# Gated DeltaNet recurrence by two groups of four heads, its beta item fifth, and the planner's clock without the residual's affine

## The chip, the cores and the metric

The kernel runs on one core of a Trainium2 chip. The metric is the device time of one execution in microseconds; three runs of the kernel before gave 1348.18, 1348.34 and 1351.75, median 1348.34. The engines are TensorE (PE, with its weight loads PEld), VectorE (DVE), ScalarE (ACT), GpSimd (POOL) and SyncE (SP). Each runs its own instructions in order and waits on semaphores for the others.

## The reference

A trunk of two layers over 512 tokens of width 1024. Layer 0 has a gated linear attention mixer, layer 1 a gated DeltaNet mixer (the one that the change touches); each is followed by a ConvFFN, and every sublayer by a LayerNorm of `ALPHA * h + f(h)`.

```python
def gdn_mixer(x, w_in, conv_w, a_log, dt_bias, norm_w, w_out):
    proj = x @ w_in
    qkv, gate, beta_lin, a_lin = jnp.split(...)
    qkv = silu(causal_dwconv(qkv, conv_w))            # 4 taps
    q, k, v = ...                                     # 8 heads of 128; q, k l2-normalized
    beta = sigmoid(beta_lin)
    g = -exp(a_log) * softplus(a_lin + dt_bias)       # per head and token
    o = rms_norm(gdn_chunked(q, k, v, beta, g), norm_w)
    return (o * silu(gate)) @ w_out

# gdn_chunked, chunk by chunk:
#   S_t = exp(g_t) (I - beta_t k_t k_t^T) S_{t-1} + beta_t k_t v_t^T ;  o_t = S_t^T q_t
```

The kernel uses chunks of 128 tokens, so the recurrence has four steps (`ck`) for each of eight heads (`hd`).

## The kernel before, in words

All activations of 512 tokens stay on the chip; weights stream in from DRAM as pieces of 128x1024, in the order of a list (`plan`), through the SP queue. ACT casts each to `wh` (L231), DVE subtracts to get the rest `wl` (L232), and each product of two fp32 matrices is three matmuls (wh with xh and xl, wl with xh).

The mixer's input projection comes first, as *items*: one item is 128 output channels by 512 tokens, 24 matmuls into one bank (`fm`). The first `HEADSTART` = 4 items are done in two halves of 256 tokens, while the LayerNorm of the last tokens is not ready; the rest is done whole. Items of the second mixer before: the beta/a item (`ba`), then q and k of head 0, 1, ... 7, then v of heads 0 to 7. Behind them come the *gates* (`tm`: tokens on the partitions, two halves `hf` of four heads, 96 matmuls each) and the output projection.

What follows an item:
- q, k, v: `gdn_conv`, one tap on ACT (L889), three on DVE (L891), Silu on ACT (L892). Then a transpose on PE (tile `qkT` or `vT`, L161), and for q and k the sums of squares on ACT (L970, into `gd_ssq`).
- beta/a (`ba_done`): Exp, softplus and a running sum (L915 to L925, ACT and DVE in turns), a store of the sums to DRAM (`drow`, L927), and eight broadcast loads from it, one per head (`dt`, L930), both on POOL's queue. `decays` then transposes beta (`bat`), subtracts on DVE (L948, four per head) and exponentiates on ACT (L953).
- `qk_task` goes on with k^T k, k^T q and the matrix `am`; `base` (two groups of four heads) inverts the triangular matrices on DVE (L1017, L1019) and PE, into `rm`.

`chain` is the recurrence. Before, one task per head, each step with 128-column operations in two shared banks, `ca` and `cb`, and a slot `cc`: transpose of k, k times state, `yy` (L1144, DVE), times `rm`, scaling (L1148, ACT), q times state, state update (L1161, DVE), output (L1163, L1164, DVE), sum of squares (L1165, ACT). Head h waits for head h - 2 at the same step, so heads run in pairs. At the last head of each step `r2` (an inverse root, L387 to L393) is made for all heads. The chains were spawned behind all items, so they ran in the gates and after them. `finish` multiplies the gated output (`sg`, L1187), and `split_y` transposes it (`yT`) for the output projection. `unspill` loads the residual `h` back and applies the last LayerNorm's affine to it on DVE (L572, L573).

The order is not written out: the parts are Python generators that are resumed by `pump` between matmuls, when a planner's clock (`clk`, advanced by each matmul's assumed cost) has passed their due time; `vec(cost)` books DVE time in that clock, and `yield t` asks to be resumed t later. `until` waits for a flag. LayerNorm's transposes (`xT`) are due when the booked DVE time is over. PE's order is fixed to the program's; a scheduler places the rows of the other engines.

Of the kernel before, what the change touches and what calls it, by code (L numbers as in the profile page):

```python
# [15 lines left out]
P = 128  # L16
# [33 lines left out]
class Trunk:  # L50
# [504 lines left out]
    def unspill(self, gb_rows):  # L555
# [339 lines left out]
    def gdn(self, li, g, b):  # L895
# [70 lines left out]
        def qk_task(t, hd, which):  # L966
            pt = self.psum("qkT")
            self.tr4(pt, t)
            for ck in range(4):
                nc.scalar.activation(pt[:, blk(ck)], pt[:, blk(ck)], AF.Square,  # L970
                                     accum_out=ssq[:, which, hd, ck:ck + 1])
            if which == 0:
                return
# [115 lines left out]
        def v_done(ps, hd):  # L1089
            if hd == 0:  # L1090
                x = self.small([P, 64], "gd_x")
                rs = self.small([P, 64], "gd_rs")
                nc.vector.tensor_scalar_add(x, ssq.rearrange("p a h c -> p (a h c)"), RMS_EPS)
                nc.vector.tensor_copy(rk, x[:, 32:].rearrange("p (h c) -> p h c", h=DH))
                self.rsqrt(rs, x, 64)
                nc.vector.tensor_copy(rr, rs[:, :32].rearrange("p (h c) -> p h c", h=DH))
                nc.vector.tensor_mul(rk, rk, rs[:, 32:].rearrange("p (h c) -> p h c", h=DH))
# [3 lines left out]
        def v_task(t, hd):  # L1101
            pt = self.psum("vT")
            self.tr4(pt, t)
            v[hd] = vt = self.slot("v")
            for ck in range(4):
                nc.scalar.mul(vt[:, blk(ck)], pt[:, blk(ck)], rk[:, hd, ck:ck + 1])
# [3 lines left out]
        items = [ba_done]  # L1110
        for hd in range(DH):
            for which in range(2):
# [3 lines left out]
        for hg in range(2):  # L1116
            self.spawn(base(hg))
        self.fm_items(items)


        ss, r2 = keep("gd_ss"), keep("gd_r2")
        sg = [[None, None] for _ in range(NTB)]
        y = [[None, None] for _ in range(NTB)]
        st = [self.slot("state"), self.slot("state")]

        def chain(hd):
            yield from self.until(("v", hd))
            yield from self.until(("rm", hd))
            yield from self.until("decays")
            s = st[hd // 4][:, blk(hd % 4)]  # L1130
            for ck in range(4):
                if ck and hd == 0:
                    yield from self.until(("chain", DH - 1, ck - 1))
                elif hd > 1:
                    yield from self.until(("chain", hd - 2, ck))
                sl = blk(ck)
                vv = v[hd][:, sl]
                pa = self.psum("ca")
                cc = self.slot("cc")
                yy, vn, kd = cc[:, blk(0)], cc[:, blk(1)], cc[:, blk(2)]  # L1140
                self.tr(pa[:, blk(0)], k[hd][:, sl])
                if ck > 0:
                    self.mm(pa[:, blk(1)], k[hd][:, sl], s)
                    nc.vector.scalar_tensor_tensor(yy, pa[:, blk(1)], neb[:, hd, ck:ck + 1], vv, ALU.mult, ALU.add)  # L1144
                nc.scalar.mul(kd, pa[:, blk(0)], ebl[:, hd, ck:ck + 1])
                yield 1.0
                self.mm(pa[:, blk(2)], rm[hd][:, sl], yy if ck else vv)
                nc.scalar.mul(vn, pa[:, blk(2)], bp[:, hd, ck:ck + 1])  # L1148
                pb = self.psum("cb")
# [127 lines left out]
```

## Time and profile before

| what | us |
|---|---|
| three runs | 1348.18, 1348.34, 1351.75 |
| profiled execution, its own time | 1347.16 |
| its span on the core | 1345.4 |
| mean granted TensorE clock | 0.988 of full speed |
| PE busy | 1302.7 |
| DVE busy | 826.6 |
| ACT busy | 551.9 |

Times below are those of the profiled execution, counted from the start of its span. The second mixer begins at about 609 us (first `fm` matmul of its head start) and ends at about 966, where the second ConvFFN's first matmul runs. A timeline row has start, duration, engine, line, operation, output<-inputs, shapes, count, and in brackets how long the engine stood idle before it and on what. Rows of the same kind in a row are joined, with their count.

### The profile page before, as it was taken

To read this page: it belongs to the slowest core of one execution; us is meant where nothing else is said; L and a number is where in the kernel's file an instruction comes from. 1 tells how busy PE (TensorE), PEld (TensorE's weight loads), DVE (VectorE), ACT (ScalarE), POOL (GpSimd) and SP (SyncE) were. 2 spreads that over 40 slices of the span, in tenths; PEclk is the share of its full clock that TensorE was granted. 3 is DMA by queue.
4 is the path that set the end of the run, shared out by engine and by line. 5 is a ranking of instruction groups with operands and counts; after the bars stand their busy time and mean duration, and the time that the engine had idled before them with its cause. 6 is when DMAs were issued, how large, how long until landed. Compare 5 with 4: busy or idle time off the path is not lost. (4 is left out here: it accounts for less than half of the span.)

```text
span 1345.4 us, 17426 instructions
## 1 busy us (share of the span) xinstructions
PE 1302.7 (97%) x6686; PEld 1078.5 (80%) x6686; DVE 826.6 (61%) x1570; ACT 551.9 (41%) x1036; POOL 118.6 (9%) x162
## 2 busy tenths in 40 slices
PE   9999999999999999998999989988899999999996
PEld 8688888988888888887787768877788888888885
DVE  3853466676533555566779894679667553355546
ACT  4644443634421344426565344553444431244420
POOL 3000000070000000001032301010025000000000
PEclk9999999999999999999999999998999999999998
DMA  6321223143223333432432322143143323333331
GB/s 188 95 78 54 72 93 111 53 131 99 94 94 95 94 94 94 122 115 87 121 93 68 87 79 77 49 141 93 34 125 94 95 94 94 96 94 94 94 109 63
DMA packets 165172, 126.38 MB, mean 94 GB/s; under 512 B 13992, under 2 KB 137706, under 8 KB 165088
## 3 DMA queue, kind: packets, MB, share of 16 engines
q1 hardware_dynamic: 159984, 115.10, 28.9%
q0 software_dynamic: 4240, 8.60, 2.1%
q10 hardware_dynamic: 864, 1.57, 0.3%
q8 instruction: 52, 0.85, 0.2%
q14 instruction: 32, 0.26, 0.1%
HBM read 119.46 MB, written 5.78 MB: 93 GB/s over the span
## 5 line engine op out<-in xcount | busy, mean ns | idle before, releaser
L232 DVE TENSOR_TENSOR wl<-raw,wh 128x1024 fp32r<-128x1024 f32 (+1 forms) x191 | 239.2, 1254 | 338.7 <-ACT wh L231 337.8
L150 PE MATMUL fm<-xh,wh 128*128 128x512 f32 (+1 forms) x1104 | 412.2, 374 | 0.3 <-ACT wh L231 0.3
L150 PE MATMUL fm<-xl,wh 128*128 128x512 f32 (+1 forms) x1104 | 408.5, 370 | 0.2 <-DVE xl L526 0.2
L150 PE MATMUL fm<-xh,wl 128*128 128x512 f32 (+1 forms) x1104 | 407.5, 370 | 0.0
L231 ACT CAST wh<-raw 128x1024 fp32r<-128x1024 f32 (+1 forms) x191 | 199.3, 1044 | 296.7 <-PE tm L150 161.2
L150 PEld LDWEIGHTS fm<-xh,wh 128*128 128x128 f32 x1104 | 208.8, 189 | 40.9 <-issue 2.3
L150 PEld LDWEIGHTS fm<-xh,wl 128*128 128x128 f32 x1104 | 208.3, 189 | 38.3 <-DVE wl L232 0.2
L150 PEld LDWEIGHTS fm<-xl,wh 128*128 128x128 f32 x1104 | 208.9, 189 | 36.9 <-DVE xl L526 0.4
L601 DVE SCALAR_TENSOR_TENSOR conv<-fm,ffn_cw,conv 128x511 f32<-128x511 f32 (+1 forms) x176 | 130.7, 746 | 3.0
L150 PE MATMUL tm<-wh,gh 128*128 128x512 f32 x288 | 112.1, 389 | 0.0
L150 PE MATMUL tm<-wl,gh 128*128 128x512 f32 x288 | 112.1, 389 | 0.0
L150 PE MATMUL tm<-wh,gl 128*128 128x512 f32 x288 | 112.1, 389 | 0.0
L150 PE MATMUL tm<-wh,xh 128*128 128x512 f32 x192 | 81.0, 422 | 0.0
L378 ACT CAST gh<-conv 128x512 fp32r<-128x512 f32 x44 | 27.3, 621 | 123.9 <-DVE conv L616 123.7
L150 PE MATMUL tm<-wh,xl 128*128 128x512 f32 x192 | 76.3, 397 | 0.0
L150 PE MATMUL tm<-wl,xh 128*128 128x512 f32 x192 | 75.7, 394 | 0.0
L611 ACT ACTIVATE conv<-conv 128x512 f32<-128x512 f32 x44 | 27.8, 632 | 92.5 <-DVE conv L601 92.5
L150 PEld LDWEIGHTS tm<-wh,gl 128*128 128x128 f32 x288 | 54.1, 188 | 11.3
L150 PEld LDWEIGHTS tm<-wh,gh 128*128 128x128 f32 x288 | 54.1, 188 | 11.3
L150 PEld LDWEIGHTS tm<-wl,gh 128*128 128x128 f32 x288 | 54.1, 188 | 11.2
L599 ACT ACTIVATE conv<-fm,ffn_cw 128x512 f32<-128x512 f32 x88 | 59.9, 681 | 0.1
L540 POOL TENSOR_TENSOR h<-h,gb 128x512 f32<-128x512 f32 x16 | 27.1, 1718 | 359.4 <-DMA gb<-in_ln_g_dram 359.4
(262 smaller groups left out, 1659.0 us busy)
## 6 DMA issues: line engine op xcount, KB each, us to landing
raw<-in_ffn_w_in_dram SPq DMA_DIRECT2D x88, 512.0 KB, 3.7
raw<-in_ffn_w_out_dram SPq DMA_DIRECT2D x44, 512.0 KB, 3.6
raw<-in_gdn_w_in_dram SPq DMA_DIRECT2D x32, 512.0 KB, 4.1
raw<-in_gla_w_in_dram SPq DMA_DIRECT2D x24, 512.0 KB, 3.6
raw<-in_gla_w_out_dram SPq DMA_DIRECT2D x8, 512.0 KB, 3.5
raw<-in_gdn_w_out_dram SPq DMA_DIRECT2D x8, 512.0 KB, 3.8
hd<-h POOLq DMA_DIRECT2D x8, 256.0 KB, 2.5
dt<-drow POOLq DMA_DIRECT2D x8, 256.0 KB, 7.0
```

The costliest lines, as they stand in the source:

```text
L150: t = self.nc.tensor.matmul(out, a, b, start=start, stop=stop)
L231: nc.scalar.copy(wh[:, cols], raw[:, cols])
L232: nc.vector.tensor_sub(wl[:, cols], raw[:, cols], wh[:, cols])
L378: cast = self.nc.scalar.copy(dst_h, src)
L540: nc.gpsimd.tensor_mul(h[hf], h[hf], gb[hf])
L599: nc.scalar.activation(a, ps, AF.Identity, scale=tap(2))
L601: nc.vector.scalar_tensor_tensor(a[:, d:], ps[:, :S - d], tap(2 - d), a[:, d:], ALU.mult, ALU.add)
L611: nc.scalar.activation(a, a, AF.Gelu)
```

## The change

Four edits:
1. The beta/a item is the fifth: the head start holds q and k of heads 0 and 1, and beta is done whole behind them.
2. `chain` is one task for a group of four heads. Each operation of a step is done for the four heads in a whole bank of its own (`ks`, `vn`, `kT`, `qs`, `s`, `o`), so the copies and additions are 512 columns wide, and k's transposes are left out in the last step. A group's task waits for its own heads alone; it is spawned ahead of the items, so that group 0 can start when v of heads 0 to 3 and their `rm` are there.
3. `r2` and the normalizers `rk`, `rr` are made per group (new flags `ssq`, `rk`, `r2`), and `finish` for half hf needs `r2` of group hf only.
4. `unspill`'s affine books no DVE time in the planner (`self.vec(1.4)` is gone).

```diff
-                    self.vec(1.4)
                     self.set(("h", tb, hf))
...
     def gdn_plan(self, w_in, w_out):
-        self.plan_pad([(w_in, 4096, 8, 0), (w_in, 4104, 8, H0)])
         for hd in range(DH):
+            if hd == HEADSTART // 2:
+                self.plan_pad([(w_in, 4096, 8, 0), (w_in, 4104, 8, H0)])
...
+            self.set(("ssq", which, hd))
...
         def v_done(ps, hd):
-            if hd == 0:
...
             t = self.gdn_conv(ps, 16 + hd)
             self.spawn(v_task(t, hd), 4.5)
         def v_task(t, hd):
+            g, h = divmod(hd, 4)
+            hs4 = slice(4 * g, 4 * g + 4)
+            if h == 0:
+                for i in range(4 * g, 4 * g + 4):
+                    yield from self.until(("ssq", 0, i))
+                    yield from self.until(("ssq", 1, i))
...
+                v[g] = [self.slot("v") for _ in range(4)]
+                self.set(("rk", g))
+            else:
+                yield from self.until(("rk", g))
...
+        def chain(g):
+            heads = [(blk(h), 4 * g + h) for h in range(4)]
+            for _, hd in heads:
+                yield from self.until(("v", hd))
+                yield from self.until(("rm", hd))
+            yield from self.until("decays")
+            s = self.slot("state")
+            for ck in range(4):
+                sl, one = blk(ck), slice(ck, ck + 1)
+                vv = yy = v[g][ck]
+                if ck > 0:
+                    ps = self.psum("ks")
+                    for w, hd in heads:
+                        self.mm(ps[:, w], k[hd][:, sl], s[:, w])
+                    yy = self.slot("yy")
+                    for w, hd in heads:
+                        nc.vector.scalar_tensor_tensor(yy[:, w], ps[:, w], neb[:, hd, one], vv[:, w],
+                                                       ALU.mult, ALU.add)
+                    yield 1.2
+                ps = self.psum("vn")
+                for w, hd in heads:
+                    self.mm(ps[:, w], rm[hd][:, sl], yy[:, w])
+                vn = self.slot("vn")
+                for w, hd in heads:
+                    nc.scalar.mul(vn[:, w], ps[:, w], bp[:, hd, one])
+                if ck < 3:
+                    ps = self.psum("kT")
+                    kd = self.slot("kd")
+                    for w, hd in heads:
+                        self.tr(ps[:, w], k[hd][:, sl])
+                    for w, hd in heads:
+                        nc.scalar.mul(kd[:, w], ps[:, w], ebl[:, hd, one])
+                if ck > 0:
+                    ps = self.psum("qs")
+                    for w, hd in heads:
+                        self.mm(ps[:, w], q[hd][:, sl], s[:, w])
+                    for w, hd in heads:
+                        nc.vector.tensor_scalar_mul(vv[:, w], ps[:, w], eb[:, hd, one])
+                yield 1.4
+                if ck < 3:
+                    ps = self.psum("s")
+                    for w, hd in heads:
+                        self.mm(ps[:, w], kd[:, w], vn[:, w])
+                    if ck == 0:
+                        nc.vector.tensor_copy(s, ps)
+                    else:
+                        for w, hd in heads:
+                            nc.vector.scalar_tensor_tensor(s[:, w], s[:, w], cd[:, hd, one], ps[:, w],
+                                                           ALU.mult, ALU.add)
+                ps = self.psum("o")
+                for w, hd in heads:
+                    self.mm(ps[:, w], pj[hd][:, sl], vn[:, w])
+                if ck == 0:
+                    nc.vector.tensor_copy(vv, ps)
+                else:
+                    nc.vector.tensor_add(vv, vv, ps)
+                for w, hd in heads:
+                    nc.scalar.activation(vn[:, w], vv[:, w], AF.Square, accum_out=ss[:, hd, one])
+                yield 1.2
...
+        def finish(tb, hf):
+            yield from self.until(("sg", tb, hf))
+            yield from self.until(("r2", hf))
...
-        items = [ba_done]
+        items = []
         for hd in range(DH):
+            if hd == HEADSTART // 2:
+                items.append(ba_done)
...
         for hg in range(2):
             self.spawn(base(hg))
+            self.spawn(chain(hg))
         self.fm_items(items)
...
-        for hd in range(DH):
-            self.spawn(chain(hd))
```

What this does to the order, at three places. The first is DVE's queue around the `dt` rows. Before, where the transposed beta (`gd_bt`) has been read and `dt_4970` (head 0) comes up; the `conv` there is k of head 1, and the convolutions of q0, k0 and q1 stand earlier:

```order
L976 RECIPROCAL gd_bp_4775<-gd_bp_4775 128x4
L977 TENSOR_TENSOR gd_bp_4775<-gd_bp_4775,gd_bt_4779 128x4
L978 TENSOR_SCALAR gd_bn_4774<-gd_bp_4775 128x4
L232 TENSOR_TENSOR wl_5203<-raw_5200,wh_5202 128x1024
L891 SCALAR_TENSOR_TENSOR conv_5148<-fm_5097,gdn_cw_177,conv_5148 128x511
L948 TENSOR_SCALAR dt_4970<-dt_4970,gd_bt_4779 128x128
L891 SCALAR_TENSOR_TENSOR conv_5148<-fm_5097,gdn_cw_177,conv_5148 128x510
```

And now (`dt_5141` and `dt_5143` are heads 0 and 1, `conv_5188` is q of head 2, `conv_5242` k of head 2):

```order
L925 SCALAR_TENSOR_TENSOR ba_4778<-reset_79,z_5129 8x512
L937 COPY gd_bt_4777<-bat_5219 128x256
L939 TENSOR_SCALAR gd_bt_4777<-gd_bt_4777 128x4x8
L940 RECIPROCAL gd_bt_4777<-gd_bt_4777 128x4x8
L978 TENSOR_TENSOR gd_bp_4773<-gd_bp_4773,gd_bt_4777 128x4 x2
L979 TENSOR_SCALAR gd_bn_4772<-gd_bp_4773 128x4 x2
L232 TENSOR_TENSOR wl_5297<-raw_5294,wh_5296 128x1024
L948 TENSOR_SCALAR dt_5141<-dt_5141,gd_bt_4777 128x128 x4
L948 TENSOR_SCALAR dt_5143<-dt_5143,gd_bt_4777 128x128 x4
L891 SCALAR_TENSOR_TENSOR conv_5188<-fm_5163,gdn_cw_177,conv_5188 128x511
L891 SCALAR_TENSOR_TENSOR conv_5242<-fm_5200,gdn_cw_177,conv_5242 128x511
L891 SCALAR_TENSOR_TENSOR conv_5188<-fm_5163,gdn_cw_177,conv_5188 128x510
```

The scan that feeds `drow`, and so the copies into `dt`, stands only a few rows ahead of the first row that reads `dt`, and two convolutions stand behind it. On PE the transpose of `conv_5188` (q2) follows the item of k2.

The second place is the end of the recurrence on DVE. Before, the roots of the last two steps (`gd_rs`, `rs_t`) for all heads, interleaved, and the products into `sg` of one token block (`sg_7118`) behind it:

```order
L392 TENSOR_TENSOR rs_t_1166_7533<-rs_t_1166_7533,gd_rs_1165_7529 128x8
L387 TENSOR_SCALAR gd_rs_1178_7596<-gd_x_1177_7595 128x8
L393 SCALAR_TENSOR_TENSOR gd_rs_1165_7529<-rs_t_1166_7533,gd_rs_1165_7529 128x8
L388 TENSOR_SCALAR gd_rs_1178_7596<-gd_rs_1178_7596 128x8
L389 TENSOR_SCALAR gd_x_1177_7595<-gd_x_1177_7595 128x8
L1177 SCALAR_TENSOR_TENSOR gd_r_1017_6653<-gd_rs_1165_7529,gd_rr_4778 128x8
L391 TENSOR_TENSOR rs_t_1179_7600<-gd_rs_1178_7596,gd_x_1177_7595 128x8
L1187 SCALAR_TENSOR_TENSOR sg_7118<-v_6147,gd_r_1017_6653,sg_7118 128x128
L1187 SCALAR_TENSOR_TENSOR sg_7118<-v_6335,gd_r_1017_6653,sg_7118 128x128
```

And now, the second half's gates (`sg_7594` to `sg_7616`), where no step and no root is left between the gate and its products:

```order
L232 TENSOR_TENSOR wl_7663<-raw_7660,wh_7662 128x1024
L647 TENSOR_TENSOR sg_7594<-sg_7594,gdn_nw_180 128x512
L1206 SCALAR_TENSOR_TENSOR sg_7594<-v_6578,gd_r_802_4785,sg_7594 128x128 x2
L647 TENSOR_TENSOR sg_7603<-sg_7603,gdn_nw_180 128x512
L1206 SCALAR_TENSOR_TENSOR sg_7594<-v_6578,gd_r_802_4785,sg_7594 128x128 x2
L1206 SCALAR_TENSOR_TENSOR sg_7603<-v_6579,gd_r_802_4785,sg_7603 128x128
L647 TENSOR_TENSOR sg_7616<-sg_7616,gdn_nw_180 128x512
```

The root of group 1 (L1196) stands seven rows ahead of `sg_7594`'s first, with four of the second half's weight casts between; the last product of group 1 stands on PE in the gates' first half.

The third place is PE at the end of the mixer. Before, the LayerNorm's transposes stand together ahead of the ConvFFN's first item (`fm_8279`):

```order
L161 MATMUL xT_8175<-ident_72,h_7735 128x128 x4
L161 MATMUL xT_8207<-ident_72,h_7727 128x128 x4
L161 MATMUL xT_8219<-ident_72,h_7737 128x128 x4
L161 MATMUL xT_8231<-ident_72,h_7729 128x128 x4
L161 MATMUL xT_8243<-ident_72,h_7739 128x128 x4
L161 MATMUL xT_8255<-ident_72,h_7731 128x128 x4
L161 MATMUL xT_8267<-ident_72,h_7741 128x128 x4
L150 MATMUL fm_8279<-xh_82,wh_7981 128x256
```

And now, where the transposes of the last token block (`xT_8194`, `xT_8212`) stand inside the second item:

```order
L150 MATMUL fm_8181<-xl_83,wh_7888 128x256
L161 MATMUL xT_8194<-ident_72,h_7642 128x128 x4
L150 MATMUL fm_8181<-xh_82,wl_7889 128x256
L161 MATMUL xT_8212<-ident_72,h_7652 128x128 x4
L150 MATMUL fm_8181<-xh_82,wh_7888 128x256
```

The other six stand still earlier, between the output projection's last tiles; all of the ConvFFN behind is in the same order as before.

More of the change, by code (lines that the diff above doesn't have):

```diff
@@ L1089, in v_done @@
         def v_done(ps, hd):
-            if hd == 0:
[L1091 to L1097, printed above, removed]
             t = self.gdn_conv(ps, 16 + hd)
@@ L1181, in finish @@
-        def finish(tb, hf):
-            yield from self.until(("sg", tb, hf))
-            yield from self.until(("r2", 3 if (hf or tb > 1) else tb))
-            t = sg[tb][hf]
-            for hd in range(4 * hf, 4 * hf + 4):
-                w = blk(hd % 4)
-                nc.vector.scalar_tensor_tensor(t[:, w], v[hd][:, blk(tb)], r2[:, hd, tb:tb + 1], t[:, w],
-                                               ALU.mult, ALU.mult)
-            yield 1.2
-            self.split_y(y, tb, hf, t)
-            self.set(("y", tb, hf), 1.5)
@@ L1198, in gdn @@
         self.gates(self.gdn_nw, P, sg)
-        self.wait(("r2", 3))
+        self.wait(("r2", 1))
         self.unspill(spilled)
```

95 lines of the change are left out of this document (36 added, 59 removed).

## The prediction

> **What bounds the kernel now.** I read the page's busy shares first, then the waits of the TensorE queue (PE) by releaser, then windows over the stretch from 600 to 1000 us, where the second mixer lies, and last the timelines of single rows there.
>
> ```profile
> PE 1302.7 (97%) x6686; PEld 1078.5 (80%) x6686; DVE 826.6 (61%) x1570; ACT 551.9 (41%) x1036; POOL 118.6 (9%) x162
> ```
>
> PE is busy 97% of the span. A change that leaves its matmuls alone can only win back idle or slow PE time, or lose more. From 590 to 1000 us PE waited for these (waiter, releaser, us in total, times, longest):
>
> ```profile
> PE qkT L161 <- ACT conv L892: 9.8, 3, 7.8
> PE yT L161 <- DVE sg L1187: 7.2, 2, 3.8
> PE vT L161 <- ACT conv L892: 4.3, 6, 1.0
> PE xT L161 <- DVE h L509: 4.0, 1, 4.0
> ```
>
> Four places: the first q and k transposes wait for their convolutions, the v transposes for theirs, the output's transposes (yT) for the recurrence, and the next feed-forward block (xT) for LayerNorm. The same by windows (us; busy time of PE, PEld, DVE, ACT, POOL; granted clock; DMA share; GB/s):
>
> ```profile
> 666.00:750.00 84.00, 81.97 (x440) 68.41 (x438) 75.50 (x195) 46.82 (x133) 22.46 (x42) 1.00 0.34 89
> 750.00:814.00 64.00, 58.37 (x445) 46.29 (x445) 55.02 (x125) 27.11 (x62) 9.27 (x17) 0.97 0.29 81
> 814.00:889.00 75.00, 75.00 (x622) 65.32 (x621) 42.45 (x131) 37.48 (x117) 6.87 (x14) 1.00 0.23 67
> 889.00:922.00 33.00, 24.91 (x130) 21.05 (x129) 30.50 (x114) 16.28 (x47) 4.81 (x9) 0.84 0.29 89
> ...
> 960.00:970.00 10.00, 5.93 (x37) 5.46 (x36) 7.44 (x22) 10.00 (x28) 0.00 (x0) 0.83 0.00 0
> ```
>
> VectorE (DVE) is busy 86 to 90% up to 814 us and only 57% in the gates (814 to 889), where PE never pauses. After the last gate matmul the recurrence is left over: PE idles 8.1 of 33 us and runs the rest at a clock of 0.84.
>
> **Durations used.** Starts that follow each other give the price of a row:
>
> ```profile
> 889.03 0.39 PE L150 MATMUL tm<-wl,xh 128*128 128x512 f32 x1
> 889.26 0.39 PE L150 MATMUL tm<-wh,xl 128*128 128x512 f32 x1
> 889.49 0.27 PE L161 MATMUL ca<-ident,conv 128*128 128x128 f32 x1
> 889.60 0.39 PE L150 MATMUL ca<-state,conv 128*128 128x128 f32 x2
> 889.82 0.27 PE L161 MATMUL ca<-ident,conv 128*128 128x128 f32 x1
> ```
>
> A 512-column matmul costs 0.23 us, a transpose 0.11, a plain fp32 128-column product 0.22 (it shows as two records). The new recurrence has the same 136 products and 24 transposes for 32: **0.9 us** of PE work less. Everything else is about waits.
>
> **Part 1, the beta item fifth.** Before, PE stood still until the first convolution's Silu, because beta's work came first on ACT and DVE:
>
> ```profile
> 633.50 1.04 ACT L231 CAST wh<-raw 128x1024 fp32r<-128x1024 f32 x1 [1.25 <-PE fm L150]
> 641.42 1.12 PE L161 MATMUL qkT<-ident,conv 128*128 128x128 f32 x4 [7.84 <-ACT conv L892]
> 642.76 0.63 PE L150 MATMUL fm<-xl,wh 128*128 128x512 f32 x1
> 643.19 0.63 PE L150 MATMUL fm<-xh,wl 128*128 128x512 f32 x1
> 662.44 0.60 PE L161 MATMUL qkT<-ident,conv 128*128 128x128 f32 x4
> ```
>
> The four head-start items end at 633.5; then 7.8 us idle, and six matmuls at 0.43 for 0.23, another 1.2. The row at 662.44 is q2's transpose, behind the items beta, q0, k0, q1, k1, q2, k2. In the changed order the same seven items lie ahead of q2's transpose, so that row is the place to compare.
>
> After, the head start (q0, k0, q1, k1) ends at 633.5 as well; q0's convolution has nothing ahead of it, and PE goes on with the transposes (4 groups of 0.45) and the beta item (24 x 0.23 = 5.6), with some 0.6 of short stalls: beta is done at about 641.4, where PE was just waking before. So far 8 to 9 us are gained. Then beta's chain runs. Its prices:
>
> ```profile
> 639.44 1.28 ACT L892 ACT_TABLE_LOAD   x1 [3.04 <-DVE conv L891]
> 627.31 0.59 ACT L915 ACTIVATE ba<-fm 8x512 f32<-8x512 f32 x1
> 627.91 0.68 ACT L917 ACTIVATE z<-fm,gdn_al 8x512 f32<-8x512 f32 x1
> 629.69 0.63 ACT L919 ACTIVATE na<-na 8x512 f32<-8x512 f32 x1
> 630.35 0.72 ACT L920 ACTIVATE na<-na,one 8x512 f32<-8x512 f32 x1
> 643.15 0.26 ACT L970 ACTIVATE qkT<-qkT 128x128 f32<-128x128 f32 x1
> 643.56 0.26 ACT L970 ACTIVATE qkT<-qkT 128x128 f32<-128x128 f32 x1
> 661.66 0.63 ACT L892 ACTIVATE conv<-conv 128x512 f32<-128x512 f32 x1 [2.48 <-DVE conv L891]
> ...
> 631.11 0.68 DVE L921 SCALAR_TENSOR_TENSOR z<-z,na 8x512 f32<-8x512 f32 x1 [0.19 <-ACT na L920]
> 631.90 0.47 DVE L924 TENSOR_SCALAR z<-z,gd_ea 8x512 f32<-8x512 f32 x1
> 632.48 1.21 DVE L925 TENSOR_TENSOR_SCAN ba<-reset,z 8x512 f32<-8x512 f32 x1
> 636.00 6.25 DVE L891 SCALAR_TENSOR_TENSOR conv<-fm,gdn_cw,conv 128x511 f32<-128x511 f32 x9
> 655.49 2.83 DVE L948 TENSOR_SCALAR dt<-dt,gd_bt 128x128 f32<-128x128 f32 x14
> ...
> 633.98 0.52 POOL L927 DMA_DIRECT2D drow<-ba  x1 [17.57 <-DVE ba L925]
> 636.32 4.25 POOL L930 DMA_DIRECT2D dt<-drow  x8 [1.82 <-issue]
> ...
> dt<-drow POOLq DMA_DIRECT2D x8, 256.0 KB, 7.0
> ```
>
> On ACT between 641.4 and the Ln: two table loads (2.6), L915, L917, L919, L920 (2.6), four L970 squares (0.41 apart, 1.6) and one weight cast (1.04), about 8 us with the hand-overs: 649.4. DVE adds L921, L924 and the scan, 2.5: **652**. Before, the scan ended at 633.69 and the second dt copy was issued at 636.32 + 0.53; with the median 7.0 to landing that is 643.9, 10.2 after the scan. After: 662.2.
>
> That wait was free before: the first L948 ran at 653.8, ten microseconds after the landing. After, the built order puts the eight L948 of the first two heads **ahead** of q2's and k2's convolutions on DVE. So: 662.2, four L948 (0.2 each, 0.8), five of six interleaved convolution rows (6.25/9 = 0.69 each, 3.5), Silu's table load 1.28 and Silu 0.63: q2 is ready at **668.4**. PE has only two items (11.2) and beta's transposes (which wait a little for the scan) to fill: it is through at about 653.5, and idles 15 us. Against 662.44 the change is 6.0 late there, plus again 1.2 at the low clock: **+7**. Behind the stall on DVE stand everything for k2 and q3; ACT's wait for q2 also holds the casts of the next weights, but those two are in hand.
>
> The Trainium skill, "DMA: Bandwidth & Descriptors", section "Latency and other measured facts", puts the fixed cost of a DMA at about 2 us. Two in a row would by that be near 4 us plus transfer, and q2 some 4 to 6 us sooner, +2 instead of +7. The trace has 7.0 for the second alone, eight being in flight at once, and the sum goes by the trace. The page "ScalarE: Activation LUTs", section "What ACT_TABLE_LOAD costs", gives 2.66 us for a table switch, load and drain; the three on this path would add 4 us. Here the Silu starts at 640.74, 1.30 after the load's start, so I count 1.3 each.
>
> Bounds for this part: -9 if q2 is not late at all; if only ACT's queue holds it (copies landed in time), the stall is about 7 and -2 is left; if the two copies land as late as the eighth (issued 3.7 later), +11. I take the walk's +7.
>
> **Part 2, the recurrence in two groups.** Group 0 now runs among the v items, group 1 in the first half of the gates. The prices of its DVE rows, 128 wide:
>
> ```profile
> L1163 DVE TENSOR_SCALAR v<-cb,gd_eb 128x128 f32<-128x128 f32 x8 | 2.8, 346 | 0.5 <-PE cb L150 0.4
> L1144 DVE SCALAR_TENSOR_TENSOR cc<-ca,gd_neb,v 128x128 f32<-128x128 f32 x7 | 2.4, 347 | 0.7 <-PE ca L150 0.6
> ```
>
> A group has 32 such rows (12 yy, 12 scalings, 8 state updates) at about 0.3 between starts, and 5 of 512 columns at 0.6: 13 us of DVE. It goes into the v items, which were already the tight stretch (750 to 814 above: DVE 55 and PE 58 busy of 64, PE idle 5.6). Summed row by row in the built order, from v0's convolution to v6's: DVE 65.8, PE 62.2; before, over v0 to v7, they were even (54 and 55). So DVE bounds there by 3.6, and each step's yy stands behind convolutions and weight casts in DVE's queue, some 2 more: **+5.5**. Ends: 0 (PE's matmuls of the group, 15.5 us, fill the idle) and +13 (the group's whole DVE time). I take the value nearer to the sums.
>
> In the gates each wide step has six 512-column matmuls (1.4) between its parts: four yy on DVE take 1.2 plus a hand-over, eight ACT scalings 2.1 against 2.7 of PE work. Nearly covered: **+1** over some 12 hand-overs.
>
> What it buys is the tail. The recurrence ends in the gates' first half, and yT of the second half needs only its own gate: 5.5 us of matmuls lie between that gate's last product and its transpose, against ACT 0.7, one 512-wide and four 128-wide DVE rows, 3.3. The 8.1 idle us of 889 to 922 go, and the low clock with them (0.16 of the 24.9 busy, 4.0), and about 1.5 of transposes that ran at half pace: **-13.5**; next late there is the output's weights, with DMA at 0.29.
>
> **Part 3, the residual's booked time.** The planner now starts LayerNorms earlier, so the xT transposes stand between the last output tiles and the head start. Of the 4.05 idle and the 0.83 clock behind it (10 us x 0.17 x 0.6 busy, 1.0) I count **-4.5**, at worst 0.
>
> **Sum:** -0.9 + 7 + 5.5 + 1 - 13.5 - 4.5 = **-5.4** against the profiled run's 1347.16 (its span 1345.4 and 1.8 around it); that run lies 1.2 under the median 1348.34. Predicted median: 1348.3 - 5.4 = 1342.9, call it **1342.5**. What a measurement here can tell from no change is 0.3%, 4.0 us.
>
> **Rivals.** (a) The dt copies do not hold q2: they land early, or the low end of part 1 holds. Speaks for it: 2.5 us of the 10.2 are issue. Then part 1 gives -9 to +2 and the sum is 1327 to 1338, with -2 likeliest: 1334. (b) Slower: the v items become bound by DVE's queue. PE, in order, waits at each of 12 hand-overs of group 0 for a row that stands behind a 2.1 us convolution and a 1.2 us cast. At 1.5 us each 18 in place of 6.5, so 1354; it decides from the point where DVE's sum passes PE's by 10 us, and the sums say 3.6. (c) No change: the tail keeps half of its wait, because the output's weights or the second gate half come late: -7 for -13.5, 1349. (d) The wide group is not through by the second gate half, since its base (the triangular inverses) ends later than before and its blocks come by DMA; then the tail merely moves, 1356.
>
> **How the numbers follow.** Forecast 0.45 (1338 to 1348), (a) 0.22, (b) 0.13, (c) 0.14, (d) 0.06. Faster by over 0.3% (under 1344.3): (a) and two thirds of the forecast, 0.53; within: a third of the forecast and most of (c), 0.28; slower (over 1352.4): 0.19. The range reaches from within (a) to just past (b): 1329 to 1355; outside stay the far ends of (a) and (d).
>
> **What would show it.** In the changed trace: PE idle before q2's transpose of 12 to 17 us with the convolutions of q2 behind L948 on DVE (right), or under 7 (wrong: part 1). DVE over 95% busy and PE idle 10 to 14 us between v0 and v7. No wait of yT over 1 us and a clock near 1.0 after the gates. xT waiting under 1.5 us. The forecast fails if beta's chain on ACT is much shorter than 11 us or dt lands within 6 us of the scan.

## The result and the profile after

| | before | after |
|---|---|---|
| median of the compared runs, us | 1348.59 | 1338.36 |
| lowest and highest, us | 1348.18, 1351.75 | 1334.57, 1338.54 |
| profiled execution, us | 1347.16 | 1338.32 |

The ratio is 0.9921, 95% interval 0.9898 to 0.9944: the changed kernel is faster, by 10.2 us between the medians. The sign was forecast and the time lies in the range, but the gain is nearly twice the forecast (10.2 for 5.4).

The changed kernel's page begins so (span; then busy time, share of the span and instructions of each engine):

```profile
span 1336.6 us, 17354 instructions
PE 1297.8 (97%) x6678; PEld 1074.2 (80%) x6678; DVE 818.2 (61%) x1526; ACT 548.3 (41%) x1030; POOL 118.5 (9%) x162
```

PE has eight instructions fewer and is still busy for 97%; its busy time fell by 4.9, more than the eight transposes (0.9) cost; the windows below show one place where the rest went, matmuls that now run at the full clock. The waits of PE from 590 to 1000 us (waiter, releaser, us in total, times, longest):

```profile
PE qkT L161 <- ACT conv L892: 17.1, 6, 11.5
PE R L150 <- DVE V L1060: 1.6, 1, 1.6
PE bat L161 <- DVE ba L925: 1.3, 1, 1.3
PE V L150 <- DMA T<-dinvt: 1.2, 2, 0.9
PE vT L161 <- ACT conv L892: 0.9, 2, 0.7
PE xT L161 <- DVE ln_t L494: 0.5, 1, 0.5
PE xT L161 <- DVE h L509: 0.5, 2, 0.3
```

The waits of yT (7.2 before) are gone, those of xT fell from 4.0 to 1.0 and those of vT from 4.3 to 0.9. The wait of the q and k transposes *grew*, from 9.8 to 17.1, and bat, R and V (beta's transpose and the inversions) wait for 4.1 where before only R did, for 1.3. The windows of the mixer (columns as in the prediction):

```profile
672.00:753.00 81.00, 76.81 (x405) 63.91 (x405) 67.59 (x187) 42.10 (x120) 20.16 (x35) 0.99 0.27 69
753.00:817.00 64.00, 58.69 (x478) 48.72 (x476) 59.46 (x153) 28.64 (x76) 12.25 (x25) 0.95 0.30 79
817.00:892.00 75.00, 74.59 (x632) 65.67 (x633) 50.45 (x153) 39.17 (x134) 10.80 (x20) 1.00 0.31 91
892.00:925.00 33.00, 33.00 (x153) 27.17 (x152) 24.33 (x46) 11.73 (x19) 0.00 (x0) 1.00 0.31 99
```

The gates reach 908.1 now, so 892 to 925 is their end and the start of the output projection with the yT transposes: no idle time and the full clock. Before, PE ran 24.9 of the 33 us behind the last gate, at 0.84; the 33 us behind it now (908 to 941) it runs without a pause at 1.00.

To see where time went, each stage gets a **loss**: for each PE row the time to the start of the next row, less the median of that time for rows of the same form in the run before, summed over the stage. It holds idle time and low clock together. The stage up to the first q transpose includes the slow matmuls right behind that wait; those behind q2's wait count to the stage after it.

| stage of PE's program | before | after | difference |
|---|---|---|---|
| ahead of the mixer (to 600 us) | 18.4 | 21.5 | +3.1 |
| to the first q transpose | 9.8 | 0.8 | -9.0 |
| from there to q2's transpose | 0.7 | 13.3 | +12.6 |
| q2's transpose to the first v transpose | 3.7 | 9.2 | +5.5 |
| v items, to the first gate matmul | 9.1 | 9.3 | +0.2 |
| gates | 3.1 | 1.6 | -1.5 |
| last gate matmul to the last yT | 14.2 | 0.0 | -14.2 |
| to the LayerNorm's last xT | 6.1 | 1.1 | -5.0 |
| rest | 1.0 | 1.4 | +0.4 |
| sum | 66.1 | 58.2 | -7.9 |

With 0.9 of matmul work less this is the 8.8 us between the two profiled executions. The +3.1 ahead of the mixer arises in identical code (last section); behind that 11.9 us were won: about 19 behind the last gate matmul, less 9 (-9.0 + 12.6 + 5.5) that the three stages around the beta item lost, and some 2 in smaller terms.

### The profile page after: what moved, and what is told of

It reads as the page before. It is cut to its first block, busy times and chain, and to the rows that moved or that the text cites. A ratio compares the mean times of both kernels' runs of the same rounds, so it can differ in the third digit from the quotient of the medians.

```text
span 1336.6 us, 17354 instructions
## 1 busy us (share of the span) xinstructions
PE 1297.8 (97%) x6678; PEld 1074.2 (80%) x6678; DVE 818.2 (61%) x1526; ACT 548.3 (41%) x1030; POOL 118.5 (9%) x162
## 4 chain that ended last, share of the span: by engine, by line
PE 77%; DVE 10%; issue 7%; DMA 3%; ACT 2%; POOL 1%; SPq 0%; DVEq 0%; POOLq 0%; ACTq 0%
PE fm L150 43%; PE tm L150 28%; DVE conv L891 2%; PE o L150 1%; DVE wl L232 1%; DVE tmp L1018 1%; DVE tt L1020 1%; DMA raw<-in_gla_w_in_dram 1%; PE R L150 1%; DMA raw<-in_ffn_w_out_dram 1%; ACT wh L231 1%; DVE ln_st L353 1%; POOL dblk L997 1%; PE V L150 1%; PE yT L161 1%
```

## The experiments

The theory after the result was: beta fifth loses some 9 us, the groups and the residual win some 19. Each run below has its own median, and its ratio to the kernel before on the same chip.

| run | median (lowest, highest), us | ratio (95%) |
|---|---|---|
| e1_beta_first | 1329.42 (1325.21, 1336.26) | 0.9865 (0.9839 to 0.9891) |
| e2_late_subtract | 1336.26 (1334.49, 1339.74) | 0.9910 (0.9893 to 0.9928) |
| e3_booked | 1339.41 (1336.88, 1342.32) | 0.9933 (0.9915 to 0.9951) |
| e6_chain_late | 1340.28 (1336.54, 1344.31) | 0.9935 (0.9914 to 0.9956) |
| e4_unbooked_alone | 1343.45 (1341.45, 1345.71) | 0.9956 (0.9939 to 0.9972) |
| e5_beta_alone | 1357.91 (1355.18, 1364.31) | 1.0068 (1.0044 to 1.0091) |
| e8_groups_alone | 1330.49 (1328.14, 1334.11) | 0.9868 (0.9846 to 0.9890) |
| e9_beta_third | 1338.73 (1333.49, 1341.72) | 0.9914 (0.9890 to 0.9938) |
| e10_transpose_later | 1327.23 (1326.83, 1336.15) | 0.9853 (0.9830 to 0.9876) |
| e10_transpose_latest | 1325.84 (1323.98, 1327.35) | 0.9828 (0.9813 to 0.9844) |
| e11_first_and_late | 1329.82 (1326.07, 1339.36) | 0.9866 (0.9838 to 0.9893) |

The medians of before beside them are 1347.78 (e1, e2, e3, e6), 1349.07 (e4, e5, e8, e9) and 1349.06 (e10, e11). The losses by stage that the text uses (columns: to q0; q0 to q2; q2 to v0; v items; gates; to the last yT; to the last xT):

```
                       to q0  q0-q2  q2-v0  v items  gates  to yT  to xT
before                   9.8    0.7    3.7      9.1    3.1   14.2    6.1
after                    0.8   13.3    9.2      9.3    1.6    0.0    1.1
e1_beta_first            9.8    0.7    4.2      7.3    2.2    0.0    1.5
e2_late_subtract         0.8    9.2    7.0     16.0    1.5    0.0    1.5
e3_booked                0.8   13.3    9.6     12.7    1.6    0.0    4.4
e6_chain_late            0.8   12.9    9.2     10.2    1.8    0.0    1.3
e4_unbooked_alone        9.8    1.4    3.9     10.4    3.1   13.8    0.4
e5_beta_alone            0.8   13.1    9.9     10.8    2.3   13.1    5.6
e8_groups_alone          9.8    0.8    4.4      7.3    2.2    0.0    3.5
e9_beta_third            1.9   13.7    7.0      7.3    2.2    0.0    1.4
e10_transpose_later     10.4    1.2    4.5      7.2    2.2    0.0    1.5
e10_transpose_latest     6.5    1.5    6.2      7.3    2.2    0.0    1.3
e11_first_and_late       9.8    1.2    4.4      7.7    1.7    0.0    1.4
```

### Beta first again, the rest of the change kept

```diff
-            if hd == HEADSTART // 2:
-                self.plan_pad([(w_in, 4096, 8, 0), (w_in, 4104, 8, H0)])
+        self.plan_pad([(w_in, 4096, 8, 0), (w_in, 4104, 8, H0)])   # ahead of the loop
...
-        items = []
+        items = [ba_done]
-            if hd == HEADSTART // 2:
-                items.append(ba_done)
```

> The changed kernel with the beta item first again; everything else stays. Theory (the move costs more than it wins: the first q transposes no longer wait 7.8 us for a convolution, but q2 waits 11.5 us, 1.2 are lost at the low clock, and the decays reach the later heads later): the time falls by 4 to 9 us against the changed kernel, to 1329 to 1335, PE idles about 8 us before the first q transpose and under 3 us before any later q or k transpose. Rival (the move wins, and what is lost up to the v items is the price of the grouped recurrence): 1338 to 1343, with the same loss between q2 and v0.

It took 1329.42, 8.9 under the changed kernel, as the theory said. The largest waits of PE, 590 to 1000 us, in this run:

```profile
PE qkT L161 <- ACT conv L891: 10.5, 4, 7.9
PE vT L161 <- ACT conv L891: 1.2, 2, 0.9
```

The wait of the q and k transposes is back at that of before (9.8), and the stages around it at their old losses. Moving the beta item was the part of the change that cost time.

### Beta fifth alone, in the kernel before

```diff
-        self.plan_pad([(w_in, 4096, 8, 0), (w_in, 4104, 8, H0)])
         for hd in range(DH):
+            if hd == HEADSTART // 2:
+                self.plan_pad([(w_in, 4096, 8, 0), (w_in, 4104, 8, H0)])
...
-        items = [ba_done]
+        items = []
         for hd in range(DH):
+            if hd == HEADSTART // 2:
+                items.append(ba_done)
```

> The kernel before with the beta item fifth, nothing else. Theory (the move is a loss of its own): PE idles under 1 us before q0's transpose and 10 to 13 us before q2's, the stretch from q2 to v0 loses 4 to 6 us more than the 3.7 of before, and the time rises by 6 to 11 us, to 1354 to 1359. Rival (it costs only together with the early groups): within 3 us of before.

1357.91 against 1349.07, 8.8 slower: the same 9 us as e1, from the other side. Its largest wait reads as the changed kernel's does:

```profile
PE qkT L161 <- ACT conv L893: 17.1, 7, 11.3
PE yT L161 <- DVE sg L1190: 7.3, 2, 4.0
PE xT L161 <- DVE h L509: 4.0, 1, 4.0
```

### The first use of the dt copies four microseconds later

The second `yield` of `decays` decides how early L948 is placed on DVE.

```diff
-            yield 10.0
+            yield 14.0
```

> The changed kernel with the subtractions in decays due 4 us later on the planner's clock, so that the three convolution rows of q2 and of k2 stand ahead of the L948 rows on DVE. Theory (the L948 rows, which wait for the dt copies, hold q2's convolution): q2's transpose comes about 4 us sooner, PE idles 7 to 8 us before it in place of 11.5, and the time falls by 3 to 5 us, to 1333 to 1335. Rival (ACT's queue holds q2: weight cast, first tap, table load): idle stays over 10.5 us and the time within 1 us.

The idle time before q2's transpose fell from 11.5 to 7.4, and no L948 stands ahead of q2's convolutions (the first ran at 676.8). So the wait for the copies was worth 4.1 us of the stall. The rest shows in the timeline of this run (start, duration, engine, line, operation; in brackets the idle time before and its releaser):

```profile
655.39 1.21 DVE L925 TENSOR_TENSOR_SCAN ba<-reset,z 8x512 f32<-8x512 f32 x1
...
658.11 1.04 ACT L231 CAST wh<-raw 128x1024 fp32r<-128x1024 f32 x1 [4.54 <-PE fm L150]
659.06 1.26 ACT L889 ACTIVATE conv<-fm,gdn_cw 128x512 f32<-128x512 f32 x2
...
659.18 1.23 DVE L232 TENSOR_TENSOR wl<-raw,wh 128x1024 fp32r<-128x1024 f32 x1 [0.46 <-ACT wh L231]
660.33 4.02 DVE L891 SCALAR_TENSOR_TENSOR conv<-fm,gdn_cw,conv 128x511 f32<-128x511 f32 x6
...
663.77 1.28 ACT L892 ACT_TABLE_LOAD   x1 [3.45 <-DVE conv L891]
...
665.75 1.12 PE L161 MATMUL qkT<-ident,conv 128*128 128x128 f32 x4 [7.44 <-ACT conv L892]
```

q2's first tap on ACT stands behind a weight cast that waits for PE, and PE had waited for the scan; its rows on DVE stand behind the scan and are interleaved with k2's, so q2's Silu comes after five rows, not three. Without the copies q2 is still late by the order behind beta's chain.

The time does not show the 4 us: 1336.26 is 2.1 under the changed kernel, and the two intervals overlap; it lies between what theory and rival asked for. The v items lost 16.0 for 9.3. Two waits grew in the whole mixer (1.2 and 1.6 in the changed kernel):

```profile
PE V L150 <- DMA T<-dinvt: 3.7, 4, 2.5
PE R L150 <- DVE V L1060: 2.5, 1, 2.5
```

The inversions of `base` hang on the decays, so a later subtraction may come out as a later wait there; this is argued. The waits are the smaller part of the 6.7 us: over the v items PE idles for 6.9 us in this run and for 4.3 in the changed kernel. The rest, some 4 us, goes with a lower clock. The window from 777 to 804 us, where the inversions and what follows them run, in the changed kernel, in this run, and in e3_booked:

```profile
777.00:804.00 27.00, 24.11 (x290) 20.19 (x289) 23.63 (x57) 11.45 (x28) 2.92 (x6) 0.87 0.20 49
777.00:804.00 27.00, 20.86 (x245) 18.37 (x244) 21.98 (x54) 6.63 (x14) 3.13 (x7) 0.62 0.22 54
777.00:804.00 27.00, 26.35 (x256) 22.05 (x253) 20.55 (x48) 9.21 (x24) 0.83 (x2) 0.68 0.13 31
```

PE's order in e3 is that of the changed kernel up to 947 us. Over the v items it idles less there (3.2 us for 4.3), and yet it loses 12.7 for 9.3, at a clock of 0.68 for 0.87 in this window. So the loss of the v items differs by 3.4 us between two executions of the same order, and a difference of that size in one profiled run need not be an effect of an edit.

### Beta third, inside the head start

```diff
         for hd in range(DH):
-            if hd == HEADSTART // 2:
-                self.plan_pad([(w_in, 4096, 8, 0), (w_in, 4104, 8, H0)])
             for base in (0, 1024):
+                if (hd, base) == (1, 0):
+                    self.plan_pad([(w_in, 4096, 8, 0), (w_in, 4104, 8, H0)])
```

(`items` changes in the same way.)

> The changed kernel with the beta item third, inside the head start, behind q0 and k0. Theory (q0's convolution must stand ahead of beta's chain, and the dt copies must have landed before a row waits for them): PE idles under 2 us before q0's transpose, the L948 rows stand behind q2's convolution, and 5 to 8 of the 9.8 us that the kernel with beta first loses there are won: 1321 to 1325. Rival (the wait moves to the transposes of k1 and q2, since the chain of table loads, Exp and Ln holds ACT and three weight casts stand behind it): 1327 to 1333.

1338.73: both missed. The early wait is gone (1.9 to q0), but 13.7 us are lost between q0 and q2, and no dt row is near. The timeline there:

```profile
641.15 0.68 DVE L921 SCALAR_TENSOR_TENSOR z<-z,na 8x512 f32<-8x512 f32 x1 [4.02 <-ACT na L920]
...
642.78 1.21 DVE L925 TENSOR_TENSOR_SCAN ba<-reset,z 8x512 f32<-8x512 f32 x1
644.02 3.50 DVE L232 TENSOR_TENSOR wl<-raw,wh 128x1024 fp32r<-128x1024 f32 x3
647.44 4.02 DVE L891 SCALAR_TENSOR_TENSOR conv<-fm,gdn_cw,conv 128x511 f32<-128x511 f32 x6
...
650.88 1.28 ACT L892 ACT_TABLE_LOAD   x1 [5.31 <-DVE conv L891]
652.18 1.15 ACT L892 ACTIVATE conv<-conv 128x512 f32<-128x512 f32 x2
...
652.86 1.11 PE L161 MATMUL qkT<-ident,conv 128*128 128x128 f32 x4 [11.13 <-ACT conv L892]
```

Beta's chain goes back and forth between ACT and DVE, and three weight casts and two convolutions stand behind its scan in both queues. A stall of 8 to 12 us appeared ahead of the transpose of the first convolution behind the chain in all three positions of beta: q0's (first, 7.8), q1's (third, 11.1) and q2's (fifth, 11.5). My rival had named this mechanism, ACT held by the chain and three casts behind it, but it put the wait at k1 and q2 instead of q1 and priced it too low.

### Beta first, the first transposes asked for later

Both start from e1 and change when `qk_task` of heads 0 and 1 is resumed:

```diff
-            self.spawn(qk_task(t, hd, which), 4.5)
+            self.spawn(qk_task(t, hd, which), 10.0 if hd < 2 else 4.5)   # e10_transpose_later; 12.0 in _latest
```

> The kernel with beta first (1329), and the transposes of heads 0 and 1 due 10 us behind their item on the planner's clock, for 4.5. PE then has k1's whole item and six matmuls more (7.0 us) ahead of q0's transpose. Theory (the 7.9 us before q0's transpose are a gap that any ready item fills; nothing behind is bound by it): idle there falls to 1 us, 6 to 9 us of the 9.8 are won, 1320 to 1324. Rival (DVE is the bound up to v0 and takes the time back, as after the beta item's move): the loss reappears before q2's transpose or up to v0, 1326 to 1330.

> The same, due 12 us behind: k1's item and q2's stand ahead of q0's transpose (11.2 us of matmuls). Theory: no idle before q0's transpose, all of the 9.8 is won, 1319 to 1322. Rival (three transposes in one place hold the banks, or DVE is the bound up to v0): 1325 to 1330.

PE's first transposes (timeline) in the run with 10.0:

```profile
648.42 1.12 PE L161 MATMUL qkT<-ident,conv 128*128 128x128 f32 x4 [8.27 <-ACT conv L891]
```

And in the run with 12.0:

```profile
648.30 1.97 PE L161 MATMUL qkT<-ident,conv 128*128 128x128 f32 x8 [2.85 <-ACT conv L891]
652.10 1.12 PE L161 MATMUL qkT<-ident,conv 128*128 128x128 f32 x4 [1.82 <-ACT conv L891]
```

Both theories missed (1320 to 1324, 1319 to 1322). With 10.0 PE takes one item more ahead of the transpose and stands just as long, because the convolutions slid with it: the first row on DVE runs at 643.00, for 636.47 in e1, and ACT's taps stand behind a weight cast that waits 5.0 us for PE. With 12.0 the wait is split and the loss up to q0 falls from 9.8 to 6.5, of which the stage from q2 to v0 gives back 2.0 (6.2 for 4.2). At 1325.84 this is the fastest kernel of the study, 1.7% under before and under both kernels compared. Against e1 its gain of 3.6 lies within overlapping intervals.

### The residual's booked time

```diff
                     # in unspill, e3: put back into the changed kernel; e4: taken out of the kernel before
+                    self.vec(1.4)
```

> The changed kernel with the 1.4 us per residual tile booked again in the planner. Theory (this edit alone moved the LayerNorm transposes): xT waits about 4 us again and the time rises by 4 to 5 us, to 1342 to 1344. Rival (the gap went because DVE is no longer busy with the recurrence's end): xT waits under 1 us and the time is the same within 1 us.

> The kernel before with the booked 1.4 us per residual tile taken out, nothing else. Theory (this edit alone moves the LayerNorm transposes, whatever the recurrence does): the loss on PE between the last yT and the ConvFFN falls from 6 to 1 or 2 us, and the time by 3 to 5 us, to 1343 to 1345. Rival (in the kernel before DVE is late with the LayerNorm itself, since the recurrence's end is still in its queue): under 1 us.

In the kernel before, taking it out wins 5.6 us (1343.45 against 1349.07), and the loss up to xT falls from 6.1 to 0.4. In the changed kernel, putting it back raises that loss from 1.1 to 4.4, with a wait that reads:

```profile
PE xT L161 <- DVE h L509: 2.4, 1, 2.4
```

Its time, 1339.41, lies between theory and rival, only 1.1 over 1338.36, which the spread does not tell from nothing. So the stage shows 3.3 us for this edit beside the groups, and the time leaves its size open.

### The groups alone

Beta first as in e1, and booked:

```diff
+                    self.vec(1.4)
```

> The changed kernel with the beta item first and the residual's time booked again, so that the grouped recurrence stands alone. Theory (parts add up): the tail is free, no loss over 1 us between the last gate and yT, xT waits about 3 us, and the time is 3 us over that of the kernel with beta first (1329), 1331 to 1334, 14 to 16 under before. Rival (the early LayerNorm is a result of the grouping): 1328 to 1330.

18.6 us under before, more than I expected: of its losses 14.2 went at the tail, 1.8 in the v items, 0.9 in the gates and 2.6 up to xT. The 2.6 come without the third edit, so part of what that edit wins alone the groups win already: with them it is worth 2.0 in the stage (3.5 in e8, 1.5 in e1) where alone it was 5.7. In time it is worth 1.1 beside the groups (1330.49 and 1329.42), which the spread does not tell from nothing, and 5.6 alone. So the parts (-18.6, +8.8, -5.6: -15.4) add up to more than the -10.2 of all together.

### The groups' tasks spawned behind the items

```diff
         for hg in range(2):
             self.spawn(base(hg))
-            self.spawn(chain(hg))
         self.fm_items(items)
+        for hg in range(2):
+            self.spawn(chain(hg))
```

> The changed kernel with both group tasks spawned behind the items, so that the recurrence runs in the gates again, but by groups of four heads. Theory (wide steps alone cure the tail, the early start costs DVE time among the v items): the stretch from v0 to v7 loses 3 to 6 us less, the tail stays free, and the time falls by 2 to 5 us, to 1333 to 1336. Rival (the early start is what cures the tail): yT waits again for 5 to 8 us behind the last gate, and the time rises to 1343 to 1350.

> The kernel with beta first, and both group tasks spawned behind the items. Theory (the recurrence among the v items costs PE nothing there, DVE has the room): same as the kernel with beta first within 2 us, 1328 to 1331, no yT wait over 1 us. Rival (the group's 13 us of DVE are the price that the prediction put on them): 1323 to 1326, and the loss from v0 to the gates falls from 7.3 us to under 4.

Now group 0 runs in the gates: its first k times state moves from 807 to 824 us in e6. Neither run differs clearly from its counterpart: 1340.28 against 1338.36 (beta fifth; both theory and rival missed), 1329.82 against 1329.42 (beta first, as the theory said). No yT wait came back, so the early start is not what cures the tail. What the traces show is a shorter recurrence. The last product of each step (count, duration in ns, first and last start), before and in e6:

```profile
L150 PE MATMUL cb<-cc,dt x64: 271/275/377, 813.5 to 906.4; 128*128 128x128 f32 x64
L150 PE MATMUL o<-vn,dt x64: 270/275/276, 821.7 to 891.2; 128*128 128x128 f32 x64
```

Before, the gates ran from 806.0 to 889.3 and the recurrence's matmuls from 807.5 to 906.4, 17 us past the last gate. In e6, with all of it among the gates too, they run from 818.0 to 891.2, 73 us for 99, and end 15 us ahead of the last gate (906.4).

The v items lose as much without group 0 as with it (10.2 and 9.3; 7.7 and 7.3). The window over the v items, in the changed kernel:

```profile
761.00:838.00 77.00, 72.72 (x658) 61.94 (x658) 67.30 (x176) 38.25 (x115) 16.59 (x33) 0.96 0.29 72
```

And in e6, where the v items end at 816.5:

```profile
758.00:816.00 58.00, 52.78 (x411) 42.06 (x409) 53.42 (x134) 22.30 (x49) 10.84 (x22) 0.94 0.30 78
```

With group 0 there DVE is busy for 67.3 of 77 us (87%) and PE idle for 4.3; without it for 53.4 of 58 (92%) and 5.2. DVE does not become the bound.

## Why the prediction was right in sign and half in size

The prediction's sum was -5.4; without the 3.1 us that were lost ahead of the mixer it was -11.9. Term by term, from the table of losses:

| term | forecast | measured |
|---|---|---|
| PE's work | -0.9 | -0.9 |
| part 1, beta fifth | +7 | +9.1 (-9.0 + 12.6 + 5.5) |
| part 2, group 0 among the v items | +5.5 | +0.2 |
| part 2, hand-overs in the gates | +1 | -1.5 |
| part 2, the tail | -13.5 | -14.2 |
| part 3, xT | -4.5 | -5.0 |

(The rest of the program adds 0.4.) The rows are stages of one pair of runs, and a stage holds more than one edit. The +0.2 of the v items is a net: beta fifth alone takes that stage from 9.1 to 10.8 (e5), the groups alone take it to 7.3 (e8), and 3.4 us of it can be clock. It says that the +5.5 did not come, not more.

**The step that failed is "DVE bounds there by 3.6, and each step's yy stands behind convolutions and weight casts in DVE's queue, some 2 more: +5.5".** I had summed DVE's and PE's rows from v0's to v6's convolution and let the larger sum set the time. The sum was right for DVE: from v0's first convolution row (757.1) to v6's (827.4) it is busy for 65.2 us, against 65.8. But PE is busy for 66.0 there, against 62.2, part of it at a low clock, so DVE's is not the larger. The step also put its 5.5 on top of the 5.6 us that PE idled there before, as if those would stay. The forecast sign, "DVE over 95% busy and PE idle 10 to 14 us", did not come: 87% (67.30 of 77) and 4.3 us in all. e6 and e11 take group 0 out of the stretch and win nothing. A reading that fits, argued only: the group brings PE as much work as DVE (15.5 against 13 us by the prediction's own numbers), so its products fill times in which the v transposes waited for convolutions. The vT waits fall from 4.3 to 1.3 with the groups alone (e8) and are 2.9 with the groups late (e11); beta fifth, with the old recurrence, takes them to 2.3 as well (e5). The prediction's lower end, 0, named this reason and is the value that e6 and e11 bear out.

**Part 1 was right in mechanism up to q2's transpose.** Its walk against the timeline of the changed kernel, whose mixer runs 3.1 us late for a reason outside it:

```profile
654.64 1.21 DVE L925 TENSOR_TENSOR_SCAN ba<-reset,z 8x512 f32<-8x512 f32 x1
...
658.20 4.25 POOL L930 DMA_DIRECT2D dt<-drow  x8 [1.54 <-DMA drow<-ba]
...
661.95 1.79 DVE L948 TENSOR_SCALAR dt<-dt,gd_bt 128x128 f32<-128x128 f32 x8 [2.30 <-DMA dt<-drow]
663.66 4.02 DVE L891 SCALAR_TENSOR_TENSOR conv<-fm,gdn_cw,conv 128x511 f32<-128x511 f32 x6
...
667.10 1.28 ACT L892 ACT_TABLE_LOAD   x1 [7.54 <-DVE conv L891]
668.40 1.15 ACT L892 ACTIVATE conv<-conv 128x512 f32<-128x512 f32 x2
...
669.08 1.11 PE L161 MATMUL qkT<-ident,conv 128*128 128x128 f32 x4 [11.53 <-ACT conv L892]
```

| step | forecast, us | measured less 3.1 |
|---|---|---|
| scan ends | 652 | 652.75 |
| second dt copy there | 662.2 | 659.74 |
| q2's transpose | 668.4 | 665.98 |
| idle before it | 15 | 11.5 |

The error of 2.4 us at q2's transpose is the copies' landing: 10.2 us after the scan by the walk, 7.0 measured (662.84 less 655.85), with the scan itself 0.75 later than in the walk. The landing times of the eight copies (timeline of L930), before:

```profile
DMA to landing us min/median/max: 6.0/7.0/7.6
```

And after:

```profile
DMA to landing us min/median/max: 3.7/6.9/7.6
```

I had used the median 7.0 for the second copy. It needed 4.1 (issued at 658.75), the first 3.7; the later ones still need up to 7.6. The Trainium skill, "DMA: Bandwidth & Descriptors", section "Latency and other measured facts", has a fixed cost of about 2 us, from which the prediction estimated q2 to come 4 to 6 us sooner than in the walk; it was 2.4 sooner, between that estimate and the walk. Up to q2's transpose part 1 thus cost 3.5 us against 662.44 before, and 1.8 of low clock on the rows behind it: 5.3, less than the forecast 7. What the walk left out came later: from there to v0 another 3.7 us were lost (5.5 less the 1.8). So the +7 came near the 9.1 by two misses of opposite sign. While PE stood, no item could be finished, and ACT's and DVE's queues ran dry behind it (the next weight cast on DVE, at 677.93, comes after 10.25 us of idling for ACT's, which had waited 5.05 for PE):

```profile
672.00:680.00 8.00, 8.00 (x36) 6.46 (x36) 2.07 (x4) 2.92 (x10) 0.00 (x0) 0.95 0.00 0
```

DVE is busy for 2.07 of 8 us there, in a stage where it is otherwise busy for 83% (67.59 of 81 in 672 to 753). A reading that fits: the stall that I counted once was paid again as DVE's lost time, in q and k transposes that wait 5.6 us for their convolutions from 673 to 762, for 2.0 in the same stage before. That the stall alone makes these waits longer was not tested by itself.

**The tail and xT** came out within 0.7 and 0.5 of their terms, with the signs asked for: no yT wait, clock 1.00, xT waits of 1.0 in all. For the tail the mechanism was right: the recurrence by groups is over before the last gate, in e6 and e11 even with the late start (73 and 74 us long, for 99). The last root of e6 runs at 896.3, ten before the last gate, so roots for all heads in one piece should have come in time too; that was not run. For xT the number was right by luck: the third edit is worth 2.0 (e8 to e1) or 3.3 (e3 to the changed kernel) in that stage beside the groups, the groups win 2.6 there without it, and the prediction had given the whole to the edit.

**The rivals.** (a), that the dt copies do not hold q2, is out: L948 waited 2.30 us for them with q2's rows behind it. Its time, 1334, was as near as the forecast's for another reason: the v items. (b) is refuted by e6 and e11 and by 4.3 us of idle time where it asked for 18 us of waits, (d) by the missing yT waits, (c) by the tail's 14.2.

## What to carry to other kernels

A serial chain that goes back and forth between two in-order engines cost its stall here ahead of the first work queued behind it; moving it moved the stall (7.8, 11.1 and 11.5 us in three positions). In the middle of a stage with a busy second engine it cost 9 us more in all, measured twice for the fifth position; that the stall is paid a second time there is the reading that fits. When work moves into a stretch that is bound by two engines in turn, count what it brings to both, and do not carry the old idle time over: work that fills the one engine's idle time while loading the other may cost nothing. Test each edit of a bundle alone: here one of three lost half of what the others won, and the change without it was 9 us faster.

## What the runs showed of the hardware

The profiled run after lost 3.1 us ahead of the mixer, in code that the change does not touch. The window from 60 to 80 us, before:

```profile
60.00:80.00 20.00, 20.00 (x101) 15.95 (x100) 19.19 (x35) 13.70 (x24) 0.00 (x0) 1.00 0.28 79
```

And after:

```profile
60.00:80.00 20.00, 20.00 (x82) 14.74 (x81) 17.68 (x31) 12.85 (x21) 0.00 (x0) 0.87 0.25 74
```

PE is busy throughout in both, but the granted clock is 0.87 and 82 matmuls were recorded for 101. The low clock sets in between 58 and 62 us (0.55 there, 1.00 from 54 to 58), right behind a wait of PE of 1.24 us at 57.8. The run before has the same wait (1.25) at the same place and keeps the full clock. Of the profiled runs only this one and e2's show it (losses of 21.5 and 22.2 up to 600 us, all others 18.4 to 19.0). The v items have a stretch of low clock too, of another length in each of three runs (0.87, 0.62 and 0.68 from 777 to 804). The times of the kernel before go with the mean granted clock of the whole run: beside e1, e2, e3 and e6, 1346.3 to 1347.8 at 0.986 to 0.989 (seven) and 1350.9 to 1351.7 at 0.983 (four); beside e10 and e11 six of eleven lie between, at 1348.9 to 1350.3 and 0.986. What sets the low clock off in one execution and not in the next was not tested. A single profiled pair can therefore be off by 3 us in code that no edit reaches.

The first two of eight copies issued in a row landed in 3.7 and 4.1 us where before they took 6.0 and 6.7 (636.32 to 642.30, 636.87 to 643.55). Before, a weight load was in flight beside them (636.11 to 643.02); after, the next weight load was issued only at 659.68, behind both. The other runs agree: with a weight load in flight beside them the first two took 5.5 and 6.3 (e1) and 5.7 and 6.8 (e9), without one 3.7 and 3.8 (e2) and 3.4 and 3.9 (e5). In e2 DVE is at work meanwhile (convolutions from 660.33 to 664.35), as in e1, so a busy DVE alone does not slow the copies. No run moves the load alone; that it makes the difference is argued from these times.
